# A two-layer diffusion trunk on one core: the residual kept token-major, with 256 weight columns moving in the output and second feed-forward products

## The chip, the cores and the metric

One core of a Trainium2 chip runs the whole program. The metric is the device time of one execution in microseconds, as the median of three runs.

## The reference

Two post-norm layers work on 512 latent tokens with 256 context tokens ahead (768 in layer 0, 512 in what is left of layer 1), model width 1024, feed-forward width 4096, all in fp32:

```
x = layer_norm(ALPHA * x + g1 * mixer(x * (1 + sc1) + sh1), ln1_g, ln1_b)
x = layer_norm(ALPHA * x + g2 * (relu(h @ w1) ** 2 @ w2), ln2_g, ln2_b)   # h = x * (1 + sc2) + sh2
```

The mixer of layer 0 is latent attention beside a bidirectional RWKV-7, that of layer 1 an RG-LRU; each ends in a product with `w_out` (1024 x 1024). `sh`, `sc` and `g` are six vectors per layer, from a product of the conditioning vector with `mod_w` (1024 x 6144); context tokens have their own.

## The kernel before

**Products.** An fp32 operand is split into two rounded parts, hi and lo, and a product is three TensorE passes: hi·hi, hi·lo, lo·hi (`mm3`, L183 to L185). A weight tile is loaded (`w_raw`, L152), its hi is made on ScalarE (L130), its lo on VectorE (L136).

**The residual** `t` lies feature-major, [128 features, 8, tokens]. `mm_residual` (from L441) makes, for each of 8 tiles m of 128 output features and each half of the tokens (384 in layer 0, 256 in layer 1), 24 matmuls with the weights stationary and the tokens moving; one VectorE instruction then does `t += psum * gate` (L450, a column of gates per partition; two where a half holds latent and context tokens).

**Layer norm.** The mean is over features, so `t` is turned on TensorE into a token-major PSUM tile (L330, 160 transposes in all), `bn_stats` reads it there (L333), ScalarE normalises it into `xn` (L357), and `ln_half` turns `xn` back (L384), makes the next product's input `hf` (ScalarE L390), splits it (`hhi` L392, `hlo` L396, a part of them on POOL), and writes the new residual from PSUM (L394). In the last of the four chunks of the feed-forward, `ln_ahead` lays the L330 transposes of the second half between products.

**Layer 1's modulation** is a filler: `mods_dve` makes the first blocks on VectorE during layer 0 (L271 to L282), `mods_spare` the rest on TensorE: a load of 512 KB (L247, tag `mraw`, two buffers), 8 fp32 products (L251), a ScalarE copy (L253), a transpose (L254) and two VectorE instructions (L256, L257). All use one PSUM bank, `md`.

**PSUM** has three `mm` banks for products, two double `tr` tiles for transposes, and the `md` bank. The input x, turned to feature-major, is spilled to DRAM early (`tsp`, L492) and read back at layer 0's output product; between the layers the residual passes through DRAM (`t_spill`, read at L1676).

**Order.** A scheduler with a timing model sets each engine's order; the program gives it emission order, fillers (`fill`, `paced`) and a few constants. SP issues nearly all loads, in order; a load whose buffer isn't free holds those behind it.

## Time and profile before

| | us |
|---|---|
| runs | 2079.30, 2084.34, 2087.86 |
| median | 2084.34 |
| profiled execution, its own time | 2087.57 |
| its span on the core | 2085.8 |
| mean granted clock, share of full | 0.963 |

The stages in the span: to about 777 the input products, RWKV and attention of layer 0; to about 880 its output product and first layer norm; to 1393 its feed-forward; to 1628 the second layer norm and layer 1's mixer; 1628 to 1705 layer 1's output product; to 2074.8 its layer norm and feed-forward; to 2085.8 the last layer norm and the stores.

### The profile page before, as it was taken

The page shows a single profiled execution, that of the slowest core. Times are in us where ns is not written, and L with a number is a line of the kernel's source. Part 1 is how long each engine was busy: PE and PEld are TensorE (multiplying, and loading weights), DVE is VectorE, ACT ScalarE, POOL GpSimd, SP SyncE. Part 2 cuts the span into 40 slices and gives each one's busy share as a digit, 9 for nine tenths or more (in the row PEclk, how much of TensorE's full clock was granted, in tenths as well). Part 3 has the DMA queues.
Part 4 walks back from the last instruction along what each step waited for, and adds up shares of the span by engine and source line. Part 5 has one row for each costly group of instructions (what it writes and reads, how often), then busy time and mean ns, then how long its engine had stood idle before and what let it go on. Part 6 is the DMA issues. An engine that isn't in the chain of part 4 may idle for free.

```text
span 2085.8 us, 39869 instructions
## 1 busy us (share of the span) xinstructions
PE 1932.2 (93%) x16130; PEld 1730.5 (83%) x16130; DVE 1257.9 (60%) x2583; ACT 852.5 (41%) x1479; POOL 283.9 (14%) x458
## 2 busy tenths in 40 slices
PE   7989888588999988999999999999989889999997
PEld 5767767466777767999999999998777779999997
DVE  4568766746666678774654333447699575444456
ACT  2555432524455443441231221334699444233242
POOL 0001222634435431100000000001000010000000
PEclk9999989889999998999999999999999999999999
DMA  9465544643423228332232222245521673333334
GB/s 348 140 190 179 146 132 117 171 115 93 125 65 91 67 67 253 101 87 84 83 103 81 61 61 61 66 126 157 151 72 56 199 196 102 98 96 94 99 102 142
DMA packets 411512, 249.21 MB, mean 119 GB/s; under 512 B 61200, under 2 KB 396096, under 8 KB 411200
## 3 DMA queue, kind: packets, MB, share of 16 engines
q1 hardware_dynamic: 408296, 243.58, 39.4%
q0 software_dynamic: 2848, 3.03, 0.7%
q8 instruction: 127, 2.08, 0.4%
q14 instruction: 57, 0.47, 0.1%
q10 hardware_dynamic: 184, 0.06, 0.0%
HBM read 209.38 MB, written 36.44 MB: 118 GB/s over the span
## 4 chain that ended last, share of the span: by engine, by line
PE 73%; DVE 10%; DMA 7%; ACT 5%; issue 2%; SPq 2%; POOL 0%; DVEq 0%; ACTq 0%; POOLq 0%
PE mm L183 18%; PE mm L184 18%; PE mm L185 18%; PE tr L183 2%; PE tr L184 1%; PE tr L185 1%; PE mm L883 1%; DVE wlo L136 1%; PE g L1393 1%; PE mm L874 1%; ACT whi L130 1%; DMA wraw<-in_l_mlp_w_dram 1%; DVE pr L1010 1%; PE g L1370 1%; DMA st<-rw_pq 1%
## 5 line engine op out<-in xcount | busy, mean ns | idle before, releaser
L183 PE MATMUL mm<-hhi,whi 128*128 128x384 f32 (+2 forms) x1504 | 491.8, 327 | 9.4 <-ACT f_k L719 6.1
L184 PE MATMUL mm<-hlo,whi 128*128 128x384 f32 (+2 forms) x1504 | 489.2, 325 | 0.6 <-DVE hlo L396 0.3
L185 PE MATMUL mm<-hhi,wlo 128*128 128x384 f32 (+2 forms) x1504 | 489.1, 325 | 0.0
L130 ACT CAST whi<-wraw 128x1024 fp32r<-128x1024 f32 x216 | 226.3, 1049 | 533.6 <-PE mm L184 444.8
L183 PE MATMUL mm<-uhi,whi 128*128 128x384 f32 (+1 forms) x1280 | 399.1, 312 | 4.6 <-DVE t L450 3.7
L185 PE MATMUL mm<-uhi,wlo 128*128 128x384 f32 (+1 forms) x1280 | 397.3, 311 | 3.6 <-DVE wlo L136 3.6
L184 PE MATMUL mm<-ulo,whi 128*128 128x384 f32 (+1 forms) x1280 | 396.7, 310 | 0.7 <-DVE ulo L136 0.7
L136 DVE TENSOR_TENSOR wlo<-wraw,whi 128x1024 fp32r<-128x1024 f32 x216 | 264.0, 1223 | 189.4 <-ACT whi L130 189.0
L183 PEld LDWEIGHTS mm<-hhi,whi 128*128 128x128 f32 x1504 | 287.8, 191 | 23.4 <-ACT f_k L719 6.3
L184 PEld LDWEIGHTS mm<-hlo,whi 128*128 128x128 f32 x1504 | 288.1, 192 | 11.6 <-DVE hlo L396 0.6
L185 PEld LDWEIGHTS mm<-hhi,wlo 128*128 128x128 f32 x1504 | 287.8, 191 | 11.4 <-issue 0.6
L183 PEld LDWEIGHTS mm<-uhi,whi 128*128 128x128 f32 x1280 | 243.0, 190 | 6.5 <-DVE t L450 4.0
L185 PEld LDWEIGHTS mm<-uhi,wlo 128*128 128x128 f32 x1280 | 243.1, 190 | 5.7 <-DVE wlo L136 4.9
L184 PEld LDWEIGHTS mm<-ulo,whi 128*128 128x128 f32 x1280 | 243.2, 190 | 1.3 <-DVE ulo L136 1.3
L450 DVE SCALAR_TENSOR_TENSOR t<-mm,g,t 128x256 f32<-128x256 f32 (+2 forms) x200 | 92.9, 481 | 226.9 <-PE mm L185 224.4
L347 POOL TENSOR_TENSOR lnrs<-lnrs,mhalf 128x1 f32<-128x1 f32 x20 | 10.7, 545 | 1007.6 <-DVE lnrs L346 1007.6
L1415 POOL TENSOR_SCALAR ds<-rv,rw_dd 64x64 f32<-64x64 f32 x176 | 85.7, 487 | 155.2 <-DVE rv L1429 144.6
L425 ACT ACTIVATE mr<-mm 128x384 f32<-128x384 f32 (+1 forms) x128 | 55.6, 434 | 83.5 <-PE mm L185 83.4
L130 ACT CAST uhi<-msq 128x384 fp32r<-128x384 f32 (+1 forms) x128 | 58.6, 458 | 75.8 <-DVE msq L427 75.8
L427 DVE SCALAR_TENSOR_TENSOR msq<-mm,mr 128x384 f32<-128x384 f32 (+1 forms) x128 | 62.3, 487 | 45.1 <-ACT mr L425 44.8
L136 DVE TENSOR_TENSOR ulo<-msq,uhi 128x384 fp32r<-128x384 f32 (+1 forms) x128 | 63.0, 492 | 33.2 <-ACT uhi L130 29.5
L1429 DVE SCALAR_TENSOR_TENSOR rv<-z,rw_dd,ds 64x64 f32<-64x64 f32 x176 | 49.7, 282 | 30.6 <-PE z L1427 25.8
(427 smaller groups left out, 2937.8 us busy)
## 6 DMA issues: line engine op xcount, KB each, us to landing
wraw<-in_l_mlp_w_dram SPq DMA_DIRECT2D x148, 512.0 KB
mraw<-in_l_mod_w_dram SPq DMA_DIRECT2D x48, 512.0 KB
wraw<-in_l_w_in_dram SPq DMA_DIRECT2D x36, 512.0 KB
wraw<-in_l_w_out_dram SPq DMA_DIRECT2D x32, 512.0 KB
mw<-in_l_mod_w_dram SPq DMA_DIRECT2D x16, 512.0 KB
wraw<-in_l_mod_w_dram SPq DMA_DIRECT2D x16, 512.0 KB
rw_pq<-pqbk SPq DMA_DIRECT2D x8, 768.0 KB
rw_bk<-pqbk SPq DMA_DIRECT2D x8, 768.0 KB
```

The costliest lines, as they stand in the source:

```text
L130: nc.scalar.copy(hi, src)
L136: e.tensor_tensor(out=lo, in0=src, in1=hi.bitcast(F32), op=ALU.subtract)
L183: nc.tensor.matmul(out, sh, mh, start=f, stop=False)
L184: nc.tensor.matmul(out, sh, ml, start=False, stop=False)
L185: ins = nc.tensor.matmul(out, sl, mh, start=False, stop=l)
L425: nc.scalar.activation(r, ps, AF.Relu)
L427: nc.vector.scalar_tensor_tensor(out=sq, in0=ps, scalar=0.0, in1=r, op0=ALU.max, op1=ALU.mult)
L450: nc.vector.scalar_tensor_tensor(out=t[:, m, x:y], in0=ps[:, x - a:y - a], scalar=g[:, m, s:s + 1], in1=t[:, m, x:y], op0=ALU.mult, op1=AL ...
L874: nc.tensor.transpose(ps[:, j * 128:(j + 1) * 128], p[:, (j0 + j) * 128:(j0 + j + 1) * 128], self.ident)
L883: nc.tensor.matmul(po[64 * e:64 * e + 64, :256], va[:, k0 // 128 + j, h * 64:(h + 1) * 64], pts[e][:, j, :], start=(j == 0), stop=(j == n ...
L1415: P.tensor_scalar(out=ds[d][H[e]], in0=rv[H[e], i, e, :], scalar1=dn[H[e]], scalar2=None, op0=ALU.mult)
L1429: V.scalar_tensor_tensor(out=rn[H[e], e, :], in0=zu[d][H[e], 1], scalar=dn[H[e]], in1=ds[d][H[e]], op0=ALU.mult, op1=ALU.add)
```

## The change

The residual lies token-major, [128 tokens, tiles, 1024]. `mm_rows` takes, for each 256 output columns f, groups of three token tiles (two in layer 1): 128 tokens' activations are stationary and 256 weight columns move, in two halves of four k each, 24 matmuls per (f, tile). VectorE then does `y = psum * gate` and `t += y`, 256 columns wide. The gate now varies along the free axis, so `gate_rows` spreads it over the partitions: for each 128 features VectorE scales the identity by the gate column, and an fp32 product with ones writes 128 columns of the `md` bank; ScalarE copies the full bank, 512 wide. There are 48 such products. `bn_stats` reads `t` itself, so the L330 transposes go; the transposes back stay. The new residual is made from `xn` by two VectorE instructions of 1024 per tile. Weight loads are [128, 4, 256], that is 1 KB rows in place of 512 B. The early spill goes; x is read token-major from the input. All `hlo` are made on VectorE.

```diff
@@ -170,6 +167,64 @@
+
+    def w_rows(self, ap, order):
+
+        for f in range(4):
+            parts = []
+            for h in range(2):
+                ks = order[4 * h:4 * h + 4]
+                raw = self.wp.tile([128, 4, 256], F32, tag="wraw", name=self.nm("wraw"), bufs=self.wbufs[0])
+                i = 0
+                while i < 4:
+                    n = next((n for n in range(1, 4 - i) if ks[i + n] != ks[i] + n), 4 - i)
+                    src = ap[128 * ks[i]:128 * (ks[i] + n), 256 * f:256 * f + 256]
+                    self.nc.sync.dma_start(raw[:, i:i + n], src.rearrange("(k p) c -> p k c", p=128))
+                    i += n
+                parts.append((ks, self.w_split(raw)))
+                self.fill()
+            yield f, parts
+
+    def mm_rows(self, t, ap, hi, lo, groups, g, order=tuple(range(8)), stats=False):
+
+        nc = self.nc
+        for f, parts in self.w_rows(ap, order):
+            c = slice(256 * f, 256 * f + 256)
+            for tiles in groups:
+                ps = {i: self.mm_ps()[:, :256] for i in tiles}
+                for h, (ks, (wh, wl)) in enumerate(parts):
+                    for i in tiles:
+                        tok = slice(128 * i, 128 * i + 128)
+                        with self.led():
+                            self.pace = self.mm3(ps[i], lambda k: (hi[:, ks[k], tok], lo[:, ks[k], tok]), lambda k: (wh[:, k, :], wl[:, k, :]),
+                                                 range(4), h == 0, h == 1)
+                for i in tiles:
+                    y = self.mt.tile([128, self.mtw], F32, tag="msq", name=self.nm("msq"), bufs=2)[:, :256]
+                    nc.vector.tensor_tensor(out=y, in0=ps[i], in1=g[:, min(i // 4, g.shape[1] - 1), c], op=ALU.mult)
+                    nc.vector.tensor_tensor(out=t[:, i, c], in0=t[:, i, c], in1=y, op=ALU.add)
+                    if stats and f % 2:
+                        self.ln_part(t, i, f // 2)
+
+    def gate_rows(self, g, n):
+
+        nc = self.nc
+        rows = self.lnw.tile([128, n, D], F32, tag="gb", name=self.nm("gb"), bufs=1)
+        for s in range(n):
+            for u in range(2):
+                ps = self.bank("md")
+                for b in range(4):
+                    d = self.mt.tile([128, self.mtw], F32, tag="mr", name=self.nm("mr"), bufs=2)[:, :128]
+                    nc.vector.tensor_scalar(out=d, in0=self.ident, scalar1=g[:, 4 * u + b, s:s + 1], scalar2=None, op0=ALU.mult)
+                    nc.tensor.matmul(ps[:, 128 * b:128 * b + 128], self.ones, d, start=True, stop=True)
+                nc.scalar.copy(rows[:, s, 512 * u:512 * u + 512], ps)
+        return rows
+
+    def ln_rows(self, l, name):
+
+        rows = self.lnw.tile([128, 2, D], F32, tag="lnw", name=self.nm("lnw"), bufs=1)
+        for i, x in enumerate("gb"):
+            self.nc.gpsimd.dma_start(rows[:, i], self.I[f"l{l}_{name}_{x}"].partition_broadcast(128))
+        return rows
 
@@ -316,59 +371,41 @@
...
+    def ln_part(self, t, i, u):
+
+        if i not in self.lnst:
+            self.lnst[i] = self.tmp.tile([128, 2, 6], F32, tag="lnst", name=self.nm("lnst"), bufs=4)
+        self.nc.vector.bn_stats(out=self.lnst[i][:, u, :], in_=t[:, i, 512 * u:512 * u + 512])
...
-        nc.scalar.activation(xn, pst, AF.Identity, bias=nmr, scale=rs[:, 0:1])
+        nc.scalar.activation(xn, t[:, i], AF.Identity, bias=nmr, scale=rs[:, 0:1])
...
@@ -390,14 +427,15 @@
                 nc.scalar.activation(hf[:, a - t0:b - t0], ps[:, a - t0:b - t0], AF.Identity, bias=B[:, k, s:s + 1], scale=G[:, k, s:s + 1])
             h = slice(t0, t0 + 128 * n)
             nc.vector.tensor_copy(hhi[:, k, h], hf)
-            m = min(128 * n, end - t0)
-            nc.vector.tensor_scalar(out=t[:, k, t0:t0 + m], in0=ps[:, :m], scalar1=gcol[:, k:k + 1], scalar2=bcol[:, k:k + 1],
-                                    op0=ALU.mult, op1=ALU.add)
-            (nc.gpsimd if k in LNP else nc.vector).tensor_tensor(out=hlo[:, k, h], in0=hf, in1=hhi[:, k, h].bitcast(F32), op=ALU.subtract)
+            nc.vector.tensor_tensor(out=hlo[:, k, h], in0=hf, in1=hhi[:, k, h].bitcast(F32), op=ALU.subtract)
+        for i, xn in zip(tiles, xns):
+            if i < end:
+                nc.vector.tensor_tensor(out=xn, in0=xn, in1=rows[:, 0], op=ALU.mult)
+                nc.vector.tensor_tensor(out=t[:, i], in0=xn, in1=rows[:, 1], op=ALU.add)
         self.lead = lead
 
 
-    def mlp(self, l, t, hhi, hlo, halves, g2, after_half):
+    def mlp(self, l, t, hhi, hlo, halves, gate, after_half):
         nc = self.nc
         w1, w2 = self.I[f"l{l}_mlp_w1"], self.I[f"l{l}_mlp_w2"]
         TT = halves[-1][1]
@@ -427,36 +465,22 @@
                     nc.vector.scalar_tensor_tensor(out=sq, in0=ps, scalar=0.0, in1=r, op0=ALU.max, op1=ALU.mult)
                     self.split(uhi[:, j, a:b], ulo[:, j, a:b], sq)
             self.lead = []
+            if ch == 0:
+                g2 = gate()
             last = ch == 3
-            for hv in ([[h] for h in halves] if last else [halves]):
-                for m, (wh, wl) in self.w_tiles(w2[ch * 1024:(ch + 1) * 1024, :]):
-                    for a, b in hv:
-                        self.mm_residual(t, m, a, b, lambda k: (wh[:, k, :], wl[:, k, :]),
-                                         lambda k: (uhi[:, k, a:b], ulo[:, k, a:b]), range(8), g2)
-                        if last and b == TT and m:
-                            self.ln_ahead(t, range(a // 128, b // 128), m - 1)
+            tiles = [list(range(a // 128, b // 128)) for a, b in halves]
+            for i, groups in enumerate([[x] for x in tiles] if last else [tiles]):
+                self.mm_rows(t, w2[ch * 1024:(ch + 1) * 1024, :], uhi, ulo, groups, g2, stats=last)
                 if last:
-                    after_half(hv[0])
-
-    def mm_residual(self, t, m, a, b, st, mv, ks, g, ps=None):
-
-        nc = self.nc
-        ps = self.mm_ps() if ps is None else ps
-        with self.led():
-            self.pace = self.mm3(ps[:, :b - a], st, mv, ks)
-        for s, (lo, hi) in enumerate(((0, NL), (NL, T))):
-            x, y = max(a, lo), min(b, hi)
...
@@ -681,21 +698,10 @@
...
+    def out_proj(self, w, t, ohi, olo, halves, g, after_half, order=(0, 1, 2, 4, 5, 6, 3, 7)):
+        for h in halves:
+            self.mm_rows(t, w, ohi, olo, [list(range(h[0] // 128, h[1] // 128))], g, order, True)
+            after_half(h)
@@ -1594,8 +1598,6 @@
...
-                    with tc.high_priority(-SPILL):
-                        x_spill = self.spill(t, T)
@@ -1624,6 +1626,8 @@
...
+            self.ones = self.tmp.tile([128, 128], F32, name="ones", bufs=1)
+            nc.gpsimd.memset(self.ones, 1.0)
@@ -1631,37 +1635,40 @@
                 tp = s1.enter_context(tc.tile_pool(name="tp", bufs=1, reuse_waits="tile"))
                 self.rows(s1)
                 self.mt = s1.enter_context(tc.tile_pool(name="mt", bufs=2, reuse_waits="tile"))
-                t = tp.tile([128, 8, T], F32, name="t_0")
+                self.lnw = s1.enter_context(tc.tile_pool(name="lnw", bufs=1, reuse_waits="tile"))
+                self.mtw = 384
+                t = tp.tile([128, 6, D], F32, name="t_0")
+                land = t.rearrange("p i c -> p (i c)").rearrange("p (k t) -> p k t", t=T)
                 ohi, olo = self.u_tile("uhi", T), self.u_tile("ulo", T)
                 for k in (0, 1, 2, 4, 5, 6, 3, 7):
-                    src = {3: self.ao, 7: self.fo}.get(k, t[:, k])
+                    src = {3: self.ao, 7: self.fo}.get(k, land[:, k])
                     if k % 4 < 3:
                         nc.sync.dma_start(src, o_scr[k])
                     self.split(ohi[:, k, :], olo[:, k, :], src, "act", OLO[k])
-                load_x = [lambda k=k: nc.sync.dma_start(t[:, k], x_spill[:, k]) for k in range(8)]
+                tok = lambda i: I["x"][0, i * 128:(i + 1) * 128, :] if i < 4 else I["ctx"][0, (i - 4) * 128:(i - 3) * 128, :]
+                load_x = [lambda i=i: nc.sync.dma_start(t[:, i], tok(i)) for i in range(6)]
                 for f in load_x[:2]:
                     f()
                 self.fillers = load_x[2:]
                 fin.close()
                 hhi, hlo = h_tiles(s0, side="right")
-                ln = lambda G, B, n, end: lambda h: self.ln_half(t, [h[0] // 128 + i for i in range(3)], hhi, hlo, G, B,
-                                                                 self.cols[f"l0_{n}_g"], self.cols[f"l0_{n}_b"], end)
-                self.out_proj(I["l0_w_out"], t, ohi, olo, halves, g1, ln(G1, B1, "ln1", T), WIDE)
+                ln = lambda G, B, rows, end: lambda h: self.ln_half(t, [h[0] // 128 + i for i in range(3)], hhi, hlo, G, B, rows, end)
+                self.out_proj(I["l0_w_out"], t, ohi, olo, halves, self.gate_rows(g1, 2), ln(G1, B1, self.ln_rows(0, "ln1"), 6))
                 spare = chain(*[self.mods_dve(1, b) for b in range(0, MODV, 2)])
                 self.fillers += [lambda: self.paced(spare)] * (MODV // 2 * 5)
                 self.fillers += [lambda b=b: run(self.mods_spare(1, [b])) for b in range(MODV, 16)]
                 lnl = []
-                t_spill = self.dram.tile([128, 8, NL], F32, name="t_spill")
+                t_spill = self.dram.tile([128, 4, D], F32, name="t_spill")
 
                 def ln2(h):
                     if not lnl:
                         self.fill(99)
-                        lnl.append(ln(*self.ln_affine(0, "ln2", 0, 1, 1, "a2_0"), "ln2", NL))
+                        lnl.append(ln(*self.ln_affine(0, "ln2", 0, 1, 1, "a2_0"), self.ln_rows(0, "ln2"), 4))
                     lnl[0](h)
-                    a, b = h[0], min(h[1], NL)
-                    nc.sync.dma_start(t_spill[:, :, a:b], t[:, :, a:b])
-
-                self.mlp(0, t, hhi, hlo, halves, g2, ln2)
+                    for i in range(h[0] // 128, min(h[1] // 128, 4)):
+                        nc.sync.dma_start(t_spill[:, i], t[:, i])
+
+                self.mlp(0, t, hhi, hlo, halves, lambda: self.gate_rows(g2, 2), ln2)
             run(self.mods_spare(1, range(max(16, MODV), MODL)))
             halves = [(0, 256), (256, NL)]
             self.hid = s0.enter_context(tc.tile_pool(name="hid1", bufs=1, reuse_waits="tile"))
@@ -1672,15 +1679,16 @@
             self.rows(s0)
             tp = s0.enter_context(tc.tile_pool(name="tp1", bufs=1, reuse_waits="tile"))
             self.mt = s0.enter_context(tc.tile_pool(name="mt1", bufs=2, reuse_waits="tile"))
-            t = tp.tile([128, 8, NL], F32, name="t_1")
+            self.lnw, self.mtw = tp, 256
+            t = tp.tile([128, 4, D], F32, name="t_1")
             nc.sync.dma_start(t, t_spill)
             two = lambda h: [h[0] // 128, h[0] // 128 + 1]
-            self.out_proj(I["l1_w_out"], t, ohi, olo, halves, g1,
-                          lambda h: self.ln_half(t, two(h), hhi, hlo, G1, B1, self.cols["l1_ln1_g"], self.cols["l1_ln1_b"]))
+            self.out_proj(I["l1_w_out"], t, ohi, olo, halves, self.gate_rows(g1, 1),
+                          lambda h, rows=self.ln_rows(1, "ln1"): self.ln_half(t, two(h), hhi, hlo, G1, B1, rows))
             gbc, bbc = tp.tile([128, D], F32, name="gbc"), tp.tile([128, D], F32, name="bbc")
             nc.gpsimd.dma_start(gbc, I["l1_ln2_g"].partition_broadcast(128))
             nc.gpsimd.dma_start(bbc, I["l1_ln2_b"].partition_broadcast(128))
-            self.mlp(1, t, hhi, hlo, halves, g2, lambda h: self.ln_out(t, two(h), gbc, bbc, out))
+            self.mlp(1, t, hhi, hlo, halves, lambda: self.gate_rows(g2, 1), lambda h: self.ln_out(t, two(h), gbc, bbc, out))
 
 
 # ---- launch: one core; inputs and outputs as the reference has them ----
```

TensorE's order at the start of layer 1's output product, before (`mm_16867` is a product, `tr` the transposes for the statistics, `md_...` a modulation block):

```order
L184 MATMUL mm_16867<-ulo_14976,whi_16863 128x256
L330 MATMUL tr_16925<-ident,t_16667 128x128
L251 MATMUL md_16389<-mraw_16387,sc 32x128 x8
L330 MATMUL tr_16946<-ident,t_16667 128x128
L185 MATMUL mm_16867<-uhi_14975,wlo_16864 128x256
L183 MATMUL mm_16867<-uhi_14975,whi_16863 128x256
```

One block stands between products there. The same place now (L306 and L309 are L251 and L254, L218 the gate products, L238 to L240 the three passes):

```order
L240 MATMUL mm_18050<-whi_18046,ulo_16239 128x256
L309 MATMUL md_17601<-ident,modrow_17610 128x128
L306 MATMUL md_17618<-mraw_17616,sc 32x128 x8
L309 MATMUL md_17618<-ident,modrow_17627 128x128
...
L306 MATMUL md_17822<-mraw_17820,sc 32x128 x8
L309 MATMUL md_17822<-ident,modrow_17831 128x128
L218 MATMUL md_17933<-mr_17934,ones 128x128
...
L218 MATMUL md_17947<-mr_17948,ones 128x128
...
L238 MATMUL mm_18051<-whi_18038,uhi_16238 128x256
```

Thirteen blocks, `md_17618` to `md_17822`, stand in a row with no product between them, ahead of the gate products; 72 of the stage's 384 matmuls stand before them and 312 behind.

SP's loads at the same place before:

```order
L152 DMA wraw_16797<-in_l_w_out_dram 128x8x128
L1676 DMA t_16667<-t_spill 128x4096
L247 DMA mraw_16370<-in_l_mod_w_dram 128x8x128
L247 DMA mraw_16387<-in_l_mod_w_dram 128x8x128
L152 DMA wraw_16829<-in_l_w_out_dram 128x8x128
L152 DMA wraw_16861<-in_l_w_out_dram 128x8x128
L247 DMA mraw_16404<-in_l_mod_w_dram 128x8x128
```

Block loads and weight loads alternate. SP's loads there now:

```order
L1684 DMA t_17930<-t_spill 128x4096
L302 DMA mraw_17633<-in_l_mod_w_dram 128x8x128
L302 DMA mraw_17650<-in_l_mod_w_dram 128x8x128
L182 DMA wraw_18181<-in_l_w_out_dram 128x3x256
L182 DMA wraw_18181<-in_l_w_out_dram 128x256
L302 DMA mraw_17667<-in_l_mod_w_dram 128x8x128
...
L302 DMA mraw_17820<-in_l_mod_w_dram 128x8x128
L182 DMA wraw_18188<-in_l_w_out_dram 128x2x256
```

Ten block loads stand in a row ahead of the next weight load.

VectorE in layer 0's second product, before:

```order
L450 SCALAR_TENSOR_TENSOR t_9086<-mm_11902,g_0_9065,t_9086 128x256
L136 TENSOR_TENSOR wlo_12078<-wraw_12075,whi_12077 128x1024
L450 SCALAR_TENSOR_TENSOR t_9086<-mm_11943,g_0_9065,t_9086 128x384
L450 SCALAR_TENSOR_TENSOR t_9086<-mm_11969,g_0_9065,t_9086 128x128
L450 SCALAR_TENSOR_TENSOR t_9086<-mm_11969,g_0_9065,t_9086 128x256
```

Three instructions serve 48 matmuls, and each frees its bank. VectorE in the same product now:

```order
L203 TENSOR_TENSOR msq_11204<-mm_11125,gb_10837 128x256
L204 TENSOR_TENSOR t_9084<-t_9084,msq_11204 128x256
L133 TENSOR_TENSOR wlo_11309<-wraw_11306,whi_11308 128x1024
L203 TENSOR_TENSOR msq_11282<-mm_11207,gb_10837 128x256
L203 TENSOR_TENSOR msq_11285<-mm_11208,gb_10837 128x256
L204 TENSOR_TENSOR t_9084<-t_9084,msq_11282 128x256
```

An L203 frees the product's bank, and what stands ahead of it on VectorE, here a weight's lo, holds it.

## Rows read from the trace of the kernel before

**Rows 1.** The page's first part: busy time by engine
```profile
PE 1932.2 (93%) x16130; PEld 1730.5 (83%) x16130; DVE 1257.9 (60%) x2583; ACT 852.5 (41%) x1479; POOL 283.9 (14%) x458
```

**Rows 2.** Windows: PE, PEld, DVE, ACT, POOL busy us (x), granted clock, DMA share, GB/s
```profile
960.00:1400.00 440.00, 440.00 (x2565) 436.41 (x2563) 192.40 (x381) 106.80 (x161) 1.05 (x2) 1.00 0.27 79
...
1628.00:1706.00 78.00, 66.13 (x637) 60.27 (x636) 50.24 (x105) 26.80 (x41) 3.86 (x6) 0.91 0.75 217
...
800.00:810.00 10.00, 7.42 (x44) 6.83 (x43) 9.97 (x27) 2.10 (x2) 0.00 (x0) 1.00 0.67 190
...
820.00:830.00 10.00, 10.00 (x59) 10.00 (x58) 7.33 (x16) 3.15 (x3) 0.00 (x0) 1.00 0.78 224
...
1645.00:1650.00 5.00, 2.61 (x12) 2.61 (x13) 1.27 (x3) 0.00 (x0) 0.00 (x0) 0.50 1.12 289
```

**Rows 3.** Timeline of TensorE, layer 0's w2: start, us, engine, line, operation
```profile
1099.70 0.34 PE L183 MATMUL mm<-uhi,whi 128*128 128x384 f32 x1
...
1103.94 0.34 PE L183 MATMUL mm<-uhi,whi 128*128 128x384 f32 x1
```

**Rows 4.** Timeline of TensorE, layer 1's w2
```profile
1949.79 0.28 PE L185 MATMUL mm<-uhi,wlo 128*128 128x256 f32 x1
...
1952.40 0.28 PE L184 MATMUL mm<-ulo,whi 128*128 128x256 f32 x1
```

**Rows 5.** Chain that ended last: start, us, what
```profile
1393.25 0.87 PE tr L330 x8
...
1028.63 0.36 PE md L282 x8
...
1462.25 4.85 DMA mraw<-in_l_mod_w_dram
...
1636.03 10.80 DMA t<-t_spill
...
1656.97 3.64 DMA wraw<-in_l_w_out_dram
```

**Rows 6.** Groups of instructions by shape: busy, mean ns | idle before
```profile
L330 PE MATMUL tr<-ident,t 128*128 128x128 f32 x160 | 28.1, 281 | 5.3 <-DVE t L450 3.4 <-DVE lnst L333 1.5 <-ACT xn L357 0.4
...
L450 DVE SCALAR_TENSOR_TENSOR t<-mm,g,t 128x384 f32<-128x384 f32 x40 | 24.7, 617 | 52.9 <-PE mm L185 52.9
...
L450 DVE SCALAR_TENSOR_TENSOR t<-mm,g,t 128x256 f32<-128x256 f32 x120 | 57.4, 479 | 79.6 <-PE mm L185 77.2 <-DMA t<-t_spill 2.3
...
L136 DVE TENSOR_TENSOR ulo<-msq,uhi 128x256 fp32r<-128x256 f32 x64 | 26.9, 420 | 7.1 <-ACT uhi L130 3.7
...
L136 DVE TENSOR_TENSOR wlo<-wraw,whi 128x1024 fp32r<-128x1024 f32 x216 | 264.0, 1223 | 189.4 <-ACT whi L130 189.0
...
L274 DVE TENSOR_SCALAR macc<-mraw,sc 128x128 f32<-128x128 f32 x32 | 7.3, 282 | 9.0 <-PE md L282 8.1 <-DMA mraw<-in_l_mod_w_dram 0.8
...
L482 ACT COPY t<-g 128x512 f32<-128x512 f32 x6 | 3.5, 586 | 13.2 <-PE g L481 8.7 <-DMA mw<-in_l_mod_w_dram 4.5
```

**Rows 7.** Timeline of one modulation block in layer 1's output product
```profile
1638.08 0.65 PE L251 MATMUL md<-mraw,sc 128*32 128x128 f32 x16
...
1638.84 0.27 ACT L253 COPY modrow<-md 128x128 f32<-128x128 f32 x1 [1.20 <-PE md L251]
...
1639.79 0.27 PE L254 MATMUL md<-ident,modrow 128*128 128x128 f32 x1
...
1640.10 0.17 DVE L256 TENSOR_REDUCE modred<-md 128x2 f32<-128x8 f32 x1 [1.74 <-PE md L254]
...
1640.32 0.64 PE L251 MATMUL md<-mraw,sc 128*32 128x128 f32 x16 [0.26 <-DVE modred L256]
```

**Rows 8.** Timeline of TensorE: first and last matmul of layer 1's output product
```profile
1628.23 0.28 PE L183 MATMUL mm<-uhi,whi 128*128 128x256 f32 x1
...
1705.03 0.28 PE L185 MATMUL mm<-uhi,wlo 128*128 128x256 f32 x1
```

**Rows 9.** Timeline of SP: the early spill of x
```profile
36.34 3.07 SPq L492 DMA_DIRECT2D tsp<-t  x4
```

72 lines of the change are left out of this document (13 added, 59 removed).

## The prediction

> **What bounds the kernel now.** I read the busy times first: TensorE is busy 93% of the span and VectorE 60% [rows 1], so the time is TensorE's work plus its gaps. The windows then show that this is an average over unlike stages [rows 2]. In layer 0's feed-forward (960 to 1400) TensorE is busy 440.0 of 440 us at full clock while VectorE is busy 192.4: each microsecond of TensorE's work put in or taken out there counts in full, and VectorE has room. At layer 0's output product VectorE is full (9.97 of 10 us from 800) and TensorE waits (7.42 busy). In layer 1's output product (1628 to 1706) TensorE is busy 66.13 of 78 us, loads take 0.75 of the DMA engines, and after a wait the clock is at half. Last I read the price of single steps in the timelines and the chain [rows 3 to 5], and of the other engines' instructions in the groups [rows 6].
>
> **The change part by part.** The sum is made against the profiled execution's own 2087.57 us, which lies 3.2 us over the median of 2084.34; I carry the difference over to the median.
>
> *Products.* In layer 0, 25 rows with 384 columns start between 1099.70 and 1103.94: 4.24 us / 24 = 176.7 ns each [rows 3]. In layer 1, 24 rows with 256 columns start between 1949.79 and 1952.40: 2.61 / 23 = 113.5 ns [rows 4]. Layer 0's output and second products have 1920 matmuls of 384 columns (384 + 1536), and become 2880 of 256: 1920 x 176.7 = 339.2 us against 2880 x 113.5 = 326.9, **-12.3**. Layer 1's count and width stay. The bounds: -12.3, and 0 if 256 columns cost in proportion there (176.7 x 256/384 = 117.8 ns). I take the measured rows.
>
> The Trainium skill, page TensorE: Matmul & The Clock Gate, section Back-to-back issue gap, speaks against this part: it gives the gap of matmuls as columns / 2.4 ns plus a fixed 2.5 ns, so narrower ones cost more per column. Estimated from that page, 384 columns take 162.5 ns and 256 take 109.2, the part comes to +2.4, and the sum to 14.7 us more. The rows above disagree with it: 0.460 ns a column at 384 and 0.443 at 256.
>
> *Transposes for the statistics.* 160 L330 transposes go [rows 6]; eight in a row take 0.87 us on the chain, 109 ns each [rows 5]. The 32 of layer 1's first norm belong to its output product, below; the other 128 give **-14.0**. If half of them lie in TensorE's waits, it is -7.
>
> *Gate rows.* 48 fp32 products of 128 columns come in. The nearest row is four fp32 products of 128 columns with a stationary operand 32 wide (L282): eight records, so two passes each, in 0.36 us [rows 5], 0.09 a product. With 128 wide a pass can't be shorter than that row's, and may be as long as a transpose, 0.109, so 0.22 a product. I take the upper end, since the stationary operand is as wide as the transpose's. 40 lie outside layer 1's output product: **+8.8** (3.6 to 8.8). Beside that lie their waits: one bank serves all, so after each four products TensorE's next four wait for a scaled identity (282 ns) and a 512-wide copy (586 ns) [rows 6]. Other products can stand between, but the first updates need the rows: **+5** (0 to 10).
>
> *Residual updates.* 200 instructions before, 200 pairs now. A pair is 479 + 420 ns by the nearest rows (from PSUM and from SBUF, 256 wide [rows 6]). In the feed-forward VectorE has 440 - 192.4 = 247.6 us free [rows 2], which covers it. In layer 0's output product it does not: the first half has 12 pairs, 10.8 us, for eight of 617 ns, 4.9, and 12 scaled identities, 3.4: 9.3 us more. VectorE has nothing free until 810 and 2.67 of 10 us at 820 [rows 2], at that share some 6 us until the norm at about 832. **+3** (0 to 9).
>
> *Banks.* Three banks take groups of 24 matmuls. Before, a bank came up for use again after two further groups, 48 x 176.7 ns = 8.5 us in layer 0 and 5.4 in layer 1. Now three tiles are worked on side by side, and the next group's first matmul falls 24 x 113.5 ns = 2.7 us after that bank's last one. Within it L203 must have run, behind whatever stands ahead on VectorE: two weight splits of 1.22 us and an update fill it. There are 80 such places. **+3** (0 to 24): most find VectorE free, as it idles more than half of the feed-forward.
>
> *Layer 1's output product.* The order puts 13 modulation blocks in a row on TensorE with no product between. 72 of the stage's 384 matmuls stand before them, 312 behind: the three banks are taken until the gate rows exist, and these wait for the `md` bank behind the blocks. One block's hand-over of the bank, matmuls to ScalarE to transpose to VectorE to the next matmuls, went from 1638.08 to 1640.32, 2.24 us [rows 7]. By loads into two buffers it would be (4.85 + 0.65) / 2 = 2.75 us with the block load of the chain, and 2.15 with a load of 3.64 us [rows 5, 7]. I take 2.35, near the hand-over, which the shorter load doesn't exceed. 13 x 2.35 = 30.5 from 1638.1 is 1668.6; gates 2.8 (eight products 1.8, a copy and an update 1.0), 1671.4; 312 x 113.5 ns = 35.4 and 32 transposes back, 3.5, 1710.3; the clock stays at half for a while after a wait, as from 1645 [rows 2], which I estimate at 2: 1712.3. The last product ended at 1705.3 before [rows 8]; by this its end is 7.0 later, and a second update of 0.4 stands in front of the norm: **+7.4** (-8 to +20). Below, since the stage waited before too (10.80 us for `t` [rows 5]); above, for the 2.75 and for weights queued on SP behind ten block loads.
>
> *The rest.* In the norms the new residual is two passes of 1024 instead of eight from PSUM, mostly behind the transposes back, and the last update doubles at the tail: **+1** (-2 to +4). The early spill, 3.07 us of issue with 3 MB behind it [rows 9], goes from a stretch in which TensorE is busy: **-1** (-8 to +8, since the scheduler reorders the first 777 us as well).
>
> Sum: -12.3 - 14.0 + 8.8 + 5 + 3 + 3 + 7.4 + 1 - 1 = **+0.9**, so 2088.5 beside the profiled execution and **2085** beside the median. What is saved on TensorE in layer 0 is spent on gates and on layer 1's chain of blocks.
>
> **The rivals.**
>
> *1, faster: 2070.* The chain of blocks costs nothing net, since that stage had 11.9 us of TensorE idle and the blocks that come early need not run later (-7.4); VectorE's filler gives way at layer 0's output product (-3); the banks never wait (-3); the gate waits are 3 and not 5 (-2). +0.9 - 15.4 = -14.5. For it: products and transposes stand in a stage that is 100% TensorE. Against it: nothing in the order lets a product run inside the chain.
>
> *2, slower: 2106.* The banks decide: at each of 80 places the update comes 0.3 us late, 24 us for the 3 above, +21.9. It decides once an L203 is issued over 2.7 us after its product, that is when two weight splits and another update stand ahead. For it: VectorE's order puts splits between updates. Against it: splits come in pairs only per 48 or 72 matmuls.
>
> *3, slower: 2096.* Layer 1's chain goes at the pace of the loads, 13 x (2.75 - 2.35) = 5.2, and the weight behind them is split only after it lands, 3.64 + 2 x 1.22 = 6.1 (the hi copy taken as long as the lo [rows 6]): +12.2 in all. For it: the ten block loads in a row on SP. Against it: SP issues that weight's load two blocks before the last one runs.
>
> *4, slower: 2098.* 256 columns cost in proportion in layer 0, so the first part gives 0 and not -12.3: +13.2. By the page named above it would be 2100. For it: the 256-column row is from layer 1. Against it: TensorE was just as full there.
>
> **How the numbers follow.** The forecast has .40: its parts are small and of both signs, and 2075 to 2095 holds them. Rival 1 has .29, as its two large gains rest on measured rows and its losses on readings of the order; rival 2 .14, rival 3 .08, rival 4 .04, and .05 is left for a first stage reordered to either side, 2060 to 2110. A measurement can tell 0.5%, 10.4 us. Faster .29 + .02 = .31; same .40; slower .14 + .08 + .04 + .03 = .29. The range reaches down past rival 1 by the 4 us its parts vary, 2066, and up to just past rival 2, 2108.
>
> **What would show it.** Right: no L330 row left; matmuls of 256 columns at about 113 ns apart in layer 0's second product, and that product still without waits and some 10 us shorter in all (1536 x 176.7 - 2304 x 113.5 ns); 48 gate products of about 0.2 us; in layer 1's output product about 30 us in which TensorE runs blocks alone at under half busy, and an end of that stage about 80 us after its start. Rival 1: that stage is no longer than 77 us. Rival 2: waits of matmuls for VectorE's L203 that add up to over 15 us. Rival 3: a block every 2.75 us and waits for `mraw`. Rival 4: 118 ns between matmuls. The prediction is wrong if the stages before 777 move by over 8 us, or the feed-forward of layer 0 does not get shorter.

## The result: 2.8% slower, and the profile after

The changed kernel took 2143.53 us (median of 4 runs, 2135.51 to 2145.5) against 2081.82 us of the kernel before on the same chip: a ratio of 1.0283, interval 1.0258 to 1.0307. Its profiled execution has a span of 2140.0 us, 54.2 more than that of before.

The two spans divide at the first and last matmul of each output and second product, read from TensorE's timelines:

| stretch, us | before | changed |
|---|---|---|
| to layer 0's output product | 789.7 | 796.7 |
| layer 0's output product | 84.5 | 91.2 |
| to the first second product | 77.4 | 75.1 |
| second products, chunks 0, 1, 2 | 68.6, 68.6, 68.0 | 73.0, 68.0, 68.8 |
| first products between them | 202.8 | 202.7 |
| second product, chunk 3, with half of the norm | 76.4 | 82.6 |
| layer 1's mixer | 192.3 | 182.1 |
| layer 1's output product | 77.1 | 112.1 |
| to its first second product | 54.3 | 57.0 |
| its chunk 0 | 43.7 | 47.3 |
| the rest | 282.5 | 283.3 |

One stage stands out: layer 1's output product is 35 us longer. The page of the profile shows it as a hole in the clock; its first part and two lines of its second (40 slices of 53.5 us, tenths):

```profile
PE 1953.6 (91%) x17026; PEld 1745.8 (82%) x17026; DVE 1337.3 (62%) x2829; ACT 862.0 (40%) x1491; POOL 275.7 (13%) x446
...
PE   7989798789999979999999999999898579999997
...
PEclk8999899799999979999999999999999589999999
```

TensorE is 21 us busier than before [rows 1], where the terms of the sum had it some 19 less (-12.3 - 17.4 + 10.6), and VectorE 79 us. In the 32nd slice, from 1658, TensorE is busy half the time, at half clock. The windows there (columns as in [rows 2]):

```profile
1640.00:1752.00 112.00, 77.50 (x671) 65.48 (x671) 58.90 (x132) 29.06 (x45) 3.25 (x6) 0.74 0.55 170
1655.00:1700.00 45.00, 20.18 (x209) 11.13 (x209) 7.23 (x33) 4.39 (x14) 0.00 (x0) 0.50 0.72 225
1655.00:1660.00 5.00, 0.48 (x1) 0.18 (x1) 1.53 (x3) 1.21 (x2) 0.00 (x0) 0.54 1.06 417
1660.00:1665.00 5.00, 0.00 (x0) 0.00 (x0) 0.00 (x0) 0.00 (x0) 0.00 (x0) 0.50 1.00 364
1700.00:1705.00 5.00, 4.33 (x19) 3.86 (x18) 3.90 (x13) 0.59 (x1) 0.00 (x0) 0.50 0.00 0
```

From 1655 to 1700 no engine is busy half its time. The timeline of TensorE, ScalarE and SP shows why, from the last product ahead of the row: the row's first three modulation blocks, then one in full, the last one, the gate products and the first product that may run:

```profile
1651.94 0.51 PE L240 MATMUL mm<-whi,ulo 128*128 128x256 f32 x3
...
1652.83 0.65 PE L306 MATMUL md<-mraw,sc 128*32 128x128 f32 x16 [0.26 <-DVE modred L311]
...
1666.40 1.08 PE L306 MATMUL md<-mraw,sc 128*32 128x128 f32 x16 [8.17 <-DMA mraw<-in_l_mod_w_dram]
...
1667.53 21.99 SPq L302 DMA_DIRECT2D mraw<-in_l_mod_w_dram  x9
...
1668.64 1.08 PE L306 MATMUL md<-mraw,sc 128*32 128x128 f32 x16 [0.26 <-DVE modred L311]
...
1672.11 1.08 PE L306 MATMUL md<-mraw,sc 128*32 128x128 f32 x16 [1.47 <-DMA mraw<-in_l_mod_w_dram]
1673.31 0.27 ACT L308 COPY modrow<-md 128x128 f32<-128x128 f32 x1 [3.19 <-PE md L306]
1673.63 0.48 PE L309 MATMUL md<-ident,modrow 128*128 128x128 f32 x1 [0.43 <-ACT modrow L308]
...
1696.75 1.08 PE L306 MATMUL md<-mraw,sc 128*32 128x128 f32 x16 [1.31 <-DMA mraw<-in_l_mod_w_dram]
...
1699.00 2.40 PE L218 MATMUL md<-mr,ones 128*128 128x128 f32 x8 [0.26 <-DVE modred L311]
...
1702.94 0.56 PE L238 MATMUL mm<-whi,uhi 128*128 128x256 f32 x1
```

From 1666.40 to 1696.75 eleven blocks pass, 2.76 us each, at half clock (a block's matmuls take 1.08 us, 0.65 in [rows 7]). Where a block's load lay ready, the next block started after 2.24 us (1666.40 to 1668.64), so it is mostly the loads that make 2.76 of it. The chain names what came before the eleven and what sets their pace:

```profile
1651.45 14.81 DMA mraw<-in_l_mod_w_dram
...
1667.53 4.45 DMA mraw<-in_l_mod_w_dram
...
1686.72 4.12 DMA mraw<-in_l_mod_w_dram
```

A block's load took 14.81 us. It ran beside these, which were issued from 1647 on, with the DMA engines full (share 1.06 and 1.00 in the windows above). The trace's DMA view gives operation, queue, count, KB and, for some, us to landing:

```profile
t<-t_spill SPq DMA_DIRECT2D x1, 2048.0 KB
...
lnw<-in_l_ln_g_dram POOLq DMA_DIRECT2D x1, 512.0 KB, 4.0
...
bbc<-in_l_ln_b_dram POOLq DMA_DIRECT2D x1, 512.0 KB, 9.6
```

The `lnw` loads are the change's own. `t` was there before too (10.80 us [rows 5]), and there too products stopped for it, but for 7.4 us; these two follow each other:

```profile
1639.67 0.28 PE L185 MATMUL mm<-uhi,wlo 128*128 128x256 f32 x1
...
1647.39 0.58 PE L183 MATMUL mm<-uhi,whi 128*128 128x256 f32 x1 [3.71 <-DVE t L450]
```

Now none ran for 50.5 us, from 1652.45 to 1702.94.

### The profile page after: what moved, and what is told of

Read it like the earlier page. It is cut to its first block, busy times and chain, and to the rows that moved or that the text cites. A ratio compares the mean times of both kernels' runs of the same rounds, so it can differ in the third digit from the quotient of the medians.

```text
span 2140.0 us, 41999 instructions
## 1 busy us (share of the span) xinstructions
PE 1953.6 (91%) x17026; PEld 1745.8 (82%) x17026; DVE 1337.3 (62%) x2829; ACT 862.0 (40%) x1491; POOL 275.7 (13%) x446
## 4 chain that ended last, share of the span: by engine, by line
PE 65%; DVE 12%; DMA 6%; ACT 5%; issue 3%; SPq 1%; POOL 0%; DVEq 0%; POOLq 0%; ACTq 0%
PE mm L238 16%; PE mm L239 16%; PE mm L240 16%; DMA mraw<-in_l_mod_w_dram 2%; PE tr L238 2%; DVE wlo L133 2%; PE mm L889 1%; PE tr L239 1%; PE mm L880 1%; PE tr L240 1%; PE g L1399 1%; PE g L1376 1%; DMA wraw<-in_l_mlp_w_dram 1%; ACT whi L127 1%; DVE pr L1016 1%
## 5 line engine op out<-in xcount | busy, mean ns | idle before, releaser
L238 PE MATMUL mm<-hhi,whi 128*128 128x384 f32 (+2 forms) x1504 | 490.9, 327 | 2.9 <-DVE msq L465 2.1
L240 PE MATMUL mm<-hhi,wlo 128*128 128x384 f32 (+2 forms) x1504 | 488.4, 325 | 0.3 <-DVE wlo L133 0.3
L239 PE MATMUL mm<-wlo,uhi 128*128 128x256 f32 x1600 | 450.6, 282 | 3.8 <-DVE wlo L133 3.6
L238 PE MATMUL mm<-whi,uhi 128*128 128x256 f32 x1600 | 449.7, 283 | 4.0 <-DVE msq L203 2.2
L240 PE MATMUL mm<-whi,ulo 128*128 128x256 f32 x1600 | 448.3, 281 | 0.0
L239 PEld LDWEIGHTS mm<-wlo,uhi 128*128 128x128 f32 x1600 | 304.3, 190 | 6.0 <-DVE wlo L133 5.6
L238 PEld LDWEIGHTS mm<-whi,uhi 128*128 128x128 f32 x1600 | 302.9, 190 | 7.1 <-issue 3.5
L240 PEld LDWEIGHTS mm<-whi,ulo 128*128 128x128 f32 x1600 | 303.7, 190 | 0.0
L238 PEld LDWEIGHTS mm<-hhi,whi 128*128 128x128 f32 x1504 | 287.9, 192 | 16.5 <-issue 2.8
L240 PEld LDWEIGHTS mm<-hhi,wlo 128*128 128x128 f32 x1504 | 287.6, 191 | 11.1 <-DVE wlo L133 0.5
L387 POOL TENSOR_TENSOR lnrs<-lnrs,mhalf 128x1 f32<-128x1 f32 x20 | 17.1, 860 | 1110.3 <-DVE lnrs L386 1063.7
L203 DVE TENSOR_TENSOR msq<-mm,gb 128x256 f32<-128x256 f32 x200 | 83.2, 420 | 101.3 <-PE mm L240 99.4
L465 DVE SCALAR_TENSOR_TENSOR msq<-mm,mr 128x384 f32<-128x384 f32 (+1 forms) x128 | 62.3, 488 | 43.9 <-ACT mr L463 43.7
L204 DVE TENSOR_TENSOR t<-t,msq 128x256 f32<-128x256 f32 x200 | 81.4, 419 | 2.6
```

Source lines behind the costliest of these rows:

```text
L203: nc.vector.tensor_tensor(out=y, in0=ps[i], in1=g[:, min(i // 4, g.shape[1] - 1), c], op=ALU.mult)
L204: nc.vector.tensor_tensor(out=t[:, i, c], in0=t[:, i, c], in1=y, op=ALU.add)
L238: nc.tensor.matmul(out, sh, mh, start=f, stop=False)
L239: nc.tensor.matmul(out, sh, ml, start=False, stop=False)
L240: ins = nc.tensor.matmul(out, sl, mh, start=False, stop=l)
L465: nc.vector.scalar_tensor_tensor(out=sq, in0=ps, scalar=0.0, in1=r, op0=ALU.max, op1=ALU.mult)
```

## The experiments

Each run was timed beside the kernel before on the same chip, whose median lay between 2083.1 and 2085.8 us.

**1. Another bank for layer 1's gate rows.**

```diff
-    def gate_rows(self, g, n):
+    def gate_rows(self, g, n, tr=False):
...
-                ps = self.bank("md")
+                ps = self.tr_ps()[:, :512] if tr else self.bank("md")
...
-            self.out_proj(I["l1_w_out"], t, ohi, olo, halves, self.gate_rows(g1, 1),
+            self.out_proj(I["l1_w_out"], t, ohi, olo, halves, self.gate_rows(g1, 1, True),
```

Expected: 

> The change with one edit: layer 1's output product takes the bank for its gate products from the transposes' pool and not from md. Theory A (the shared md bank puts 13 modulation blocks in a row ahead of all products, at 2.2 to 3.4 us each, much of it at half clock): the blocks lie between products again, the stage from the first to the last product of layer 1's output product falls from 112 us to 75 to 87, and the time from 2143.5 to 2108 to 2120. Theory B (the blocks only fill a wait that loads of t and of the weights set anyway): the stage falls by less than 8 us, the time stays over 2135.

Measured: 2111.32 us, ratio 1.0133 (1.0101 to 1.0164): 32 us of the 62 are gone. The stage lasts 81.8 us. In the window that stood still, and at the stage's ends:

```profile
1655.00:1700.00 45.00, 34.43 (x291) 30.60 (x295) 24.37 (x65) 15.78 (x24) 1.08 (x2) 0.81 0.76 247
...
1640.17 0.28 PE L238 MATMUL mm<-whi,uhi 128*128 128x256 f32 x1
...
1721.65 0.28 PE L240 MATMUL mm<-whi,ulo 128*128 128x256 f32 x1
```

Only the bank of eight products changed, and the blocks lie between products again, one at a time and once three. Theory A holds: the loads are the same, so they did not set the wait by themselves.

**2. The early spill put back.**

```diff
...
+                    with tc.high_priority(-SPILL):
+                        x_spill = self.spill(t, T)
```

Expected: 

> The change with the early spill of x to DRAM put back; nothing reads it. Theory A (the spill's absence reorders the first stage, which costs the 7 us by which layer 0's output product starts later): its first product starts at 788 to 792 us again and not at 796.7, the time falls by some 6 us to 2137. Theory B (the delay has another cause, such as the residual's new buffers or the token-major loads): it starts at 795 or later, the time is within 3 us of 2143.5.

Measured: 2146.69 us, ratio 1.0297 (1.0268 to 1.0326); layer 0's output product starts at 797.3. Theory A falls. VectorE's and SP's order of the first stage is now that of before, and its time isn't. But the kernel before with the edit of experiment 3, which also has that order, started this product at 781.1 in one execution and 789.1 in another: the first stage scatters by 8 us with one order. What can be told apart is the last step, from VectorE's first `ulo` of the product's input to the first product: 4.2 us in all four profiles with the old form, 8.0 in the changed kernel, here and in experiments 1, 5, 6, 7, 9 and 10 (8.7 in 4, 12.0 in 8). By this, 3.8 of the 7.0 us in the table are the change's; the rest can't be told from the scatter.

**3. 256 columns in the kernel before.**

```diff
-            for hv in ([[h] for h in halves] if last else [halves]):
+            for hv in ([[h] for h in halves] if last else [[(a, a + 256) for a in range(0, TT, 256)]]):
```

Expected: 

> The kernel before with one edit: in the first three of layer 0's four chunks the second product moves 256 tokens at a time and not 384, weights stationary as before; 1152 matmuls of 384 become 1728 of 256. Theory A (the term of the prediction, 113.5 ns against 176.7): 1152 x 176.7 - 1728 x 113.5 = 7.4 us less, 2074. Theory B (256 columns run at 117.8 ns once an fp32 product has come between, which in layer 0 is nearly always so): no gain, 2080 to 2083, and the spacing in the second product is 117 to 118 ns after a modulation block.

Measured: 2076.4 us, ratio 0.9956 (0.9931 to 0.9981). Run again for a narrower interval. Expected: 

> The kernel before with 256 columns in layer 0's first three second products, run again for its interval. Theory A (the gain is real, 6.0 us by the stages of the profile): 4 to 9 us less than before. Theory B (the 9 us of the first run were the first stage's scatter): within 3 us of before.

Measured: 2078.78 us, ratio 0.9969 (0.9953 to 0.9985). The three second products took 66.2, 67.5 and 65.5 us in both profiles, 6.0 less than before. Theory A holds: narrower columns alone gain most of what the term said (7.4 for these), and this version is 0.3% faster than the kernel before. Its chunk 1, at 67.5 us, gained little: more than half of it ran at about 118 ns.

Then the first products of chunks 1 to 3 as well.

```diff
-            order = [(j, halves) for j in range(8)]
+            thirds = [(a, a + 256) for a in range(0, TT, 256)]
+            order = [(j, thirds) for j in range(8)]
```

Expected: 

> The kernel before with 256 columns in layer 0's first three second products, as already run (ratio 0.9969 and 0.9956), and besides in the first products of the chunks 1 to 3 (576 matmuls of 384 become 864... per chunk 384 of 384 become 576 of 256). Theory A (256 columns cost 113.3 ns in one of the two paces against 173.3 to 176.7): 384 x 173.3 - 576 x 113.3 = 1.3 to 2.6 us less per chunk, 4 to 8 us beyond that run, ratio 0.993 to 0.995. Theory B (the first products fall into the 117 ns pace, as they do in layer 1): 576 x 117.5 = 67.7 us per chunk against 66.5, ratio 0.996 to 0.999.

Measured: 2082.34 us, ratio 0.9989 (0.9972 to 1.0006). Theory B: in chunk 3, where nothing stands between them, these products run at 116.7 ns (67.09 us / 575).

**4. Layer 0's gate rows by DMA** (with experiment 1's bank).

```diff
...
+        nc.tensor.transpose(ps[:16, :128], g.rearrange("p b s -> p (b s)"), self.ident)
...
+        nc.scalar.copy(row[:16, :], ps[:16, :128])
+        nc.gpsimd.dma_start(d, row[:16, :])
+        for s in range(n):
+            nc.gpsimd.dma_start(rows[:, s].rearrange("p (b c) -> p b c", c=128), d.rearrange("(b s) c -> s b c", s=2)[s].partition_broadcast(128))
```

Expected: 

> As the run with the other bank in layer 1, and besides layer 0's gate rows are spread by a DMA (one transpose, a write to DRAM, a load to all 128 partitions) and not by 32 fp32 products. Theory A (the gate products and what waits for their bank cost what the trace suggests: 4.3 us in the first chunk's second product, some 4 of the 6.6 in layer 0's output product): 6 to 10 us less than the run with the other bank. Theory B (the products are hidden, or the DMA's latency takes their place): within 3 us of it.

Measured: 2110.21 us, ratio 1.014 (1.0099 to 1.0181), no different from experiment 1 in total, which is Theory B. By stage it is both: chunk 0's second product 67.4 us and not 73.0, layer 0's output product 91.3 and not 91.0.

**5. A longer cover for the norms** (on top of 1). `lead` is the list that makes each next unit of products wait for one of the norm's transposes.

```diff
-        xns, lead = [self.ln_stats_norm(t, i) for i in tiles], [None] * (len(tiles) - 1)
+        xns, lead = [self.ln_stats_norm(t, i) for i in tiles], [None] * (5 if tiles[0] == 0 else len(tiles))
...
-                lead.append(ins)
+                lead += [ins] * (2 if tiles[0] == 0 else 1)
```

Expected: 

> As the run with the other bank in layer 1 (2111.3 us), with one edit in the norms: the list that holds products back behind the norm's transposes was kept from a time when its unit was 24 matmuls (4.2 us in layer 0); the unit is now 12 (1.4 us). After a first half five units instead of two (layer 0) or one (layer 1) go ahead freely and each further step covers two units; after a second half one unit more goes ahead. Theory A (the norm's chain from statistics to the first transpose lies bare on TensorE because the cover shrank: 91 against 84.5 us in layer 0's output product, 82.6 against 76.4 in the last chunk, 81.8 against 77.1 in layer 1's output product, 58.1 against 54.3 behind it): 8 to 15 us less, 2096 to 2103. Theory B (VectorE is late there, with the pairs of updates and hlo, so the order doesn't matter): within 3 us of 2111.

Measured: 2103.67 us, ratio 1.0096 (1.0079 to 1.0113), 7.7 less than experiment 1. In chunk 3 the same place in the changed kernel and here:

```profile
1415.00:1420.00 5.00, 2.65 (x31) 1.53 (x24) 0.55 (x3) 2.61 (x5) 0.25 (x1) 0.64 0.92 262
```

```profile
1415.00:1420.00 5.00, 5.00 (x51) 4.33 (x50) 3.55 (x9) 3.66 (x6) 0.00 (x0) 1.00 0.47 135
```

Layer 0's output product fell by 2.7 us, chunk 3 by 5.8, layer 1's output product by 5.9. That is 14.4, more than the time: the mixer took 193.1 us in this profile, 181.8 in experiment 1's and 184 to 187 in the three profiles below, and that part is not explained (this profile is of the longest of the four executions, 2110.09 us). Nor is all of chunk 3's 5.8 us shown to be the cover's: it held some three modulation blocks and not six, the others having moved into the mixer. Theory A holds, just under its low end.

**6. hlo on GpSimd again** (on top of 5).

```diff
-            nc.vector.tensor_tensor(out=hlo[:, k, h], in0=hf, in1=hhi[:, k, h].bitcast(F32), op=ALU.subtract)
+            (nc.gpsimd if k in (1, 3, 5) else nc.vector).tensor_tensor(out=hlo[:, k, h], in0=hf, in1=hhi[:, k, h].bitcast(F32), op=ALU.subtract)
```

Expected: 

> As the run with the longer cover, and hlo of k = 1, 3, 5 on GpSimd again as in the kernel before. Theory A (VectorE's work in the norms is on the path): 2 to 5 us less than that run. Theory B (it is not): within 2 us, or slower, since GpSimd took 1015 ns for one where VectorE took 545.

Measured: 2104.27 us, ratio 1.0101 (1.0084 to 1.0117). Theory B.

**7. DMA gate rows in layer 0's feed-forward alone** (on top of 5).

```diff
-                self.mlp(0, t, hhi, hlo, halves, lambda: self.gate_rows(g2, 2), ln2)
+                self.mlp(0, t, hhi, hlo, halves, lambda: self.gate_rows_dma(g2, 2), ln2)
```

Expected: 

> As the run with the longer cover, and the gate rows of layer 0's feed-forward are spread by a DMA. Theory A (16 gate products and the slower pace of 117.8 ns that follows an fp32 product cost 5.6 us in the first chunk, as 73.0 against 67.4 us showed): 4 to 7 us less than that run, 67 to 68 us from the first to the last matmul of that chunk's second product. Theory B (the earlier 5.6 was a matter of that run): 71 us or more.

Measured: 2097.1 us, ratio 1.006 (1.0039 to 1.0081), 6.6 less; chunk 0 took 67.4 us. Theory A: 16 gate products cost 5.6 us there, 0.35 each, the slower pace behind them included.

**8. No gates** (on top of 5). This kernel leaves out the gates.

```diff
...
-                    nc.vector.tensor_tensor(out=y, in0=ps[i], in1=g[:, min(i // 4, g.shape[1] - 1), c], op=ALU.mult)
-                    nc.vector.tensor_tensor(out=t[:, i, c], in0=t[:, i, c], in1=y, op=ALU.add)
+                    nc.vector.tensor_tensor(out=t[:, i, c], in0=t[:, i, c], in1=ps[i], op=ALU.add)
...
```

Expected: 

> As the run with the longer cover, but the gate is left out of both residual sums: no gate rows are made and the update is one VectorE instruction, t += psum. Theory A (gates cost their products, the waits for them and the pace): 10 to 16 us less than the run with the longer cover, most of it in the two first chunks' second products (5.6 and 2) and in the two output products. Theory B (only the products count, 48 x 0.22 us): 8 to 10 us less, spread by their number.

Measured: 2086.7 us, ratio 1.0021 (1.0005 to 1.0036), 17.0 less than experiment 5. Layer 0's output product takes 77.5 us and not 88.3, chunk 0 67.4 and not 73.0. Theory A, a little beyond its range; layer 1's output product went the other way, 79.4 us and not 75.9. Gates with their waits cost 17 us; what is left of the change, with its two faults mended, is 0.2% slower than the kernel before. Against that kernel's profile, this one's first product of layer 0's output product starts 9.4 us later, the way from there to the end of the mixer is 20.4 us shorter, and layer 1 from its output product on is 10.3 us longer.

**9. Is it VectorE in layer 0's output product?** (on top of 7)

```diff
...
-                    nc.vector.tensor_tensor(out=t[:, i, c], in0=t[:, i, c], in1=y, op=ALU.add)
+                    (nc.gpsimd if stats and g.shape[1] == 2 and self.early else nc.vector).tensor_tensor(out=t[:, i, c], in0=t[:, i, c], in1=y, op=ALU.add)
...
```

Expected: 

> As the run with the longer cover and the DMA gate rows (2097.1 us), with t += y of layer 0's output product on GpSimd; 24 instructions leave VectorE. Theory A (VectorE bounds that stage: without gates it took 77.5 us, with them 88.3 to 88.6): the stage falls to 81 to 85 us and the time by 4 to 7. Theory B (the stage waits for the gate rows and not for VectorE's pairs): it stays at 87 to 89 us.

Measured: 2097.23 us, ratio 1.006 (1.0037 to 1.0084); the stage took 90.0 us, beyond both theories' ranges, on the side of B. GpSimd did the updates:

```profile
L204 POOL TENSOR_TENSOR t<-t,msq 128x256 f32<-128x256 f32 x23 | 25.0, 1096 | 61.6 <-DVE msq L203 46.2 <-DMA wraw<-in_l_w_out_dram 11.5 <-issue 3.9
```

Each took 1096 ns and not 417, so the edit put a slower step in place of the queue; VectorE's busy time from 800 to 890 fell from 72.0 to 66.2 us and the stage gained nothing. Experiment 4 took the gate products out of this stage and this one the updates off VectorE, but each put something else in their place (a DMA; GpSimd at 1096 ns), so which of them holds the 10.8 us that gates cost there is open.

**10. No fp32 products in layer 0's feed-forward** (on top of 7). This kernel leaves out 32 of layer 1's modulation blocks.

```diff
-                spare = chain(*[self.mods_dve(1, b) for b in range(0, MODV, 2)])
...
+                nc.gpsimd.memset(self.mod[1], 0.0)
...
-            run(self.mods_spare(1, range(max(16, MODV), MODL)))
```

Expected: 

> As the run with the longer cover and the DMA gate rows, but blocks 0 to 31 of layer 1's modulation are left out (zeros stand for them), so that no fp32 product falls into layer 0's feed-forward. What is read is the pace there, not the total. Theory A (the pace of 256 columns is 113.3 ns until an fp32 product comes between and 117.8 ns from there on): all three first chunks' second products run at 113.3 ns, 576 x 113.3 = 65.3 us from first to last matmul, against 67.4, 68.0 and 68.8. Theory B (the pace changes for another cause, such as the buffers that are read): they stay at 67 to 69 us with 117.8 ns in them.

Measured in one execution: second products of 65.4, 68.0 and 65.4 us. Every row of TensorE in chunk 1 and in chunk 2 stands at one pace; the first and last of 25 rows in each:

```profile
1099.74 0.28 PE L253 MATMUL mm<-wlo,uhi 128*128 128x256 f32 x1
...
1102.57 0.28 PE L253 MATMUL mm<-wlo,uhi 128*128 128x256 f32 x1
...
1233.79 0.28 PE L252 MATMUL mm<-whi,uhi 128*128 128x256 f32 x1
...
1236.51 0.28 PE L252 MATMUL mm<-whi,uhi 128*128 128x256 f32 x1
```

2.83 / 24 = 117.9 ns and 2.72 / 24 = 113.3 ns, for the same instructions at full clock. Theory A holds for two chunks, and with nothing between, the pace does not change. But chunk 1 took the slow one from its start, without an fp32 product: the fp32 product is one thing that changes the pace and not the only one.

## Why the prediction was wrong, step by step

The forecast was no change, 2085 within 2066 to 2108; 2143.5 lies outside. Three steps failed: the size of layer 1's chain of blocks, the cover of the norms, which the sum put at nothing, and the -26.3 of products and transposes, which did not reach the total. The price of gates came out near. One sign of being wrong that the prediction named came true: layer 0's feed-forward, from its first second product to the end of chunk 3, is 10.8 us longer.

**Layer 1's output product, +7.4 (-8 to +20).** The mechanism was right: the blocks stood in a row, no product ran among them, and a bank was the cause, as experiment 1 shows. The size was not: the stage grew by 35 us. The first product behind the blocks was put 43 us after the stage's start (1671.4); it came at 1702.9, 62.6 us after. Of these 19.5 us, 11.2 are one wait, the 13.57 us between the blocks at 1652.83 and 1666.40 where a step of 2.35 was forecast. The row for the load of `t` was read (10.80 us), but as something that the stage had always waited for; a block's load that stands beside it was not priced, and with no product to run TensorE stood still for it. Another 4.5 are the pace of the eleven blocks that followed. It was that of the loads, which stood under rival 3: 2.75 us forecast for it, 2.76 measured, in part by luck, since loads of 4.0 to 4.5 us and not 4.85 met matmuls of 1.08 us and not 0.65. Behind the blocks the stage took 49.5 us and not 40.9: the granted clock, priced at 2 us, was half from about 1655 to past 1705, and TensorE waited 5.0 us in all for the norm's `xn`, most of it here:

```profile
1725.28 0.69 PE L421 MATMUL tr<-ident,xn 128*128 128x128 f32 x2 [4.46 <-ACT xn L397]
```

The mixer ahead of the stage is 10 us shorter than before, but not as the other side of this fault: it took 181.8 us in experiment 1 too, where the blocks are no longer in a row. Some 10 modulation blocks lay in it in both and 15 before, yet with one block, in experiment 10, it took 185.1; the cause is open. So the fault cost 30 us of the stage and 32 of the time.

**The rest, +1 for the norms.** Here the step that failed was one that the text did not price: the products that may run ahead of a norm's transposes. The list counts units, two or one of them; a unit had been 24 matmuls and now is 12, so in layer 0 the cover fell from 2 x 24 x 176.7 = 8.5 us to 2 x 12 x 117.8 = 2.8. The group of the transposes back, before (L384) and now (L421), shows the bare wait, beside the gate products:

```profile
L384 PE MATMUL tr<-ident,xn 128*128 128x128 f32 x128 | 18.6, 278 | 5.9 <-ACT xn L357 5.8
...
L421 PE MATMUL tr<-ident,xn 128*128 128x128 f32 x128 | 23.0, 317 | 17.7 <-ACT xn L397 17.7
L218 PE MATMUL md<-mr,ones 128*128 128x128 f32 x96 | 20.0, 321 | 4.2 <-DVE mr L217 2.3 <-ACT gb L219 1.7 <-DVE modred L311 0.3
```

That is 17.7 us of waiting for `xn` and 5.9 before. Experiment 5, which lengthens the cover, took 7.7 us out of the time.

**Products, -12.3 (-12.3 to 0).** The end at 0 came nearly true in the second products, and at the pace given for it, 117.8 ns, but not because 256 columns cost so in layer 0: both prices exist there. In chunk 2 of the changed kernel, 26 rows before a modulation block at 1256, then 25 rows behind it:

```profile
1249.87 0.28 PE L238 MATMUL mm<-whi,uhi 128*128 128x256 f32 x1
...
1252.70 0.28 PE L239 MATMUL mm<-wlo,uhi 128*128 128x256 f32 x1
...
1257.93 0.28 PE L239 MATMUL mm<-wlo,uhi 128*128 128x256 f32 x1
...
1260.76 0.28 PE L239 MATMUL mm<-wlo,uhi 128*128 128x256 f32 x1
```

2.83 / 25 = 113.2 ns, and 2.83 / 24 = 117.9. From there to the end of the chunk it stays. So chunks 1 and 2 gained 0.6 and lost 0.8 us where 2.5 each was forecast, and layer 1's later second products stand at 45.4 us in experiments 7 and 8, where 43.7 was the time before. In the kernel before the same width runs mostly at the fast pace, and gains (experiment 3). In its chunk 0 an fp32 product leaves it so:

```profile
986.10 0.43 PE L282 MATMUL md<-macc,ones 128*32 128x128 f32 x8
...
990.34 0.28 PE L185 MATMUL mm<-uhi,wlo 128*128 128x256 f32 x1
...
993.06 0.28 PE L185 MATMUL mm<-uhi,wlo 128*128 128x256 f32 x1
```

2.72 / 24 = 113.3 ns. The new form of the stream, activations stationary, falls into the slow pace more often. That the form itself is the cause is not shown: experiment 10 has it at the fast pace in two chunks, and the old form runs at the slow one in experiment 3's chunk 1. The rule on the gap of matmuls, which the Trainium skill gives on the page TensorE: Matmul & The Clock Gate (section Back-to-back issue gap) and calls there that of a single matmul, would put 256 columns at an estimated 109.2 ns and 384 at 162.5. Neither pace here is as short, and experiment 3 gained where by that rule it would have lost.

**Gates, +8.8, +5 and +3.** Products, waits and pairs came to 16.8 by the sum, and 2.8 more stood in layer 1's term; experiment 8 measures 17.0 for all of them. That is near, but in part by luck, as the parts are not as they were put. The 48 products were busy for 20.0 us, 0.42 each where 0.22 was put, at half clock in places. Yet two in a row between products at full clock passed in 0.36 us, below what was put:

```profile
971.04 0.60 PE L218 MATMUL md<-mr,ones 128*128 128x128 f32 x4
971.40 0.36 PE L239 MATMUL mm<-wlo,uhi 128*128 128x256 f32 x1
```

And the 10.8 us in layer 0's output product are not shown to be VectorE's.

**Transposes, -14.0, and what became of the savings.** All 160 are gone. With gates out and both faults mended, the terms left in the sum are -12.3 - 14.0 + 3 + 1 - 1 = -23.3; experiment 8 measures +3.6 (2086.7 against 2083.1). Its profile shows where it went: the 20.4 us gained from the start of layer 0's output product to that of layer 1's were spent ahead of them (9.4, of which 7.8 in the step from VectorE's first `ulo` to the first product) and in layer 1 (10.3). Of those, 1.7 us on each of three second products are the slow pace; the waits behind the rest are not told apart.

**Banks, +3 (0 to 24).** Right: TensorE waited 2.2 us in all for an L203 to free a bank, so rival 2 had no part in it.

**Rival 4**, 2098, rested on 118 ns between matmuls, which is mostly what was seen. **Rival 1** took the chain of blocks to cost nothing; it cost the most. **Rival 3** had the chain's pace, but not the one long wait.
